# Two-layer hybrid attention block: three engines tied to the planner's order in both attention stages, rotations ahead of the values, a fourth raw weight buffer

## The chip, the core and the metric

The kernel runs on one core of one Trainium2 chip. The metric is device microseconds from the first to the last instruction of one execution. The core's engines are named as in the profile: PE (TensorE: matrix products and transposes), DVE (VectorE), ACT (ScalarE), POOL (GpSimd) and SP (SyncE, which here only issues DMAs). Each engine works through its own list of instructions in the order in which the program gives them; an instruction that waits for another engine holds up everything behind it in its list.

## The reference

512 latent tokens and 256 context tokens, both of width 1024, go through two layers. Each layer modulates its input, runs a token mixer, adds with a gate, normalises, and does the same around a squared-ReLU MLP. Cut to the two mixers:

```python
# layer 0: 16 query heads over 2 key/value heads of 64, a window of 3 blocks of 128 keys plus all 256 context keys
q = apply_rope((hx @ wq)...);  k = apply_rope((hx @ wk)...);  v = (hx @ wv)...
p = softmax_with_sink(concat([s_lat, s_ctx]), sink);  o = p @ [v, vc]

# layer 1: 8 heads of differential attention over 512 + 256 keys; no output for the context tokens
q = apply_rope((hx @ wq).reshape(B, L, H, 2, d)); k = apply_rope(...); v = (hx @ wv).reshape(B, L, H, 2 * d)
p = softmax(s);  a = p[:, :, 0] - lam * p[:, :, 1];  o = a @ v_all
o = o * rsqrt(mean(o * o)) * subln_g * (1 - lam_init)
```

`apply_rope` rotates the two halves of each head of queries and keys by tables of cosines and sines; values are not rotated, and neither is anything of the context tokens.

## The kernel before, in words

Every float32 product is made of three products of rounded numbers: a matrix is split into a high part (ScalarE rounds it) and a low part (VectorE subtracts the high part from the original), and `mm3` (L324) adds high·high, high·low and low·high. So each weight tile is loaded by a DMA into a "raw" buffer, rounded by ScalarE (`w_h`) and subtracted by VectorE (`w_l`, L314): this is `wsplit` (L301). Three raw buffers (`NRAW`, L39) go round; a load waits until the subtraction that last used its buffer is done. The helper `split` (L506) does the same to activations. The helpers `dv`, `ac` and `gp` issue on VectorE, ScalarE and GpSimd, and most of their work stands in the profile under their lines L260, L264 and L268.

**Four stages** follow each other: attention of layer 0, MLP of layer 0, attention of layer 1, MLP of layer 1. The stage of layer 0 starts with the conditioning products (`ada_ps`), key/value projection (`kv_ps`, `kv_job` L1173, `kv_post` L1224), query projection (`q_ps`, `proj` L1284, `q_post` L1255), then 24 groups of 4 heads and one block of 128 tokens (`group`, L1322): scores `s_ps`, VectorE's mask-and-minimum `nm`, ScalarE's exponential, VectorE's reciprocal, GpSimd's scaling, transposes `pT_ps`, product with the values `o_ps`.

The stage of layer 1 goes head by head. `proj1` (L1685) splits the head's four weight tiles and computes, for six blocks of 128 tokens (four latent, two context), `qkv_ps` with queries, keys and values of that head side by side in one PSUM tile. `post1` (L1632) then works on each block: it splits the values into `vt`, rotates queries and keys (`rope`, L488: three VectorE products into `rope` buffers and one GpSimd addition), splits the keys into `sk` and the queries into `sq`, and TensorE transposes them (`kT_ps`, `qT_ps`); ScalarE copies the results to `kS` and `qT`. In the code of before, `post1` issues the split of the values first and the rotation behind it; for a context block there is no rotation, and the split of the values stands ahead of that of the keys. `scores1` (L1746) makes the scores, `nm`, the exponentials `e` and, from the two maps of a head, VectorE's combination `e<-e,nl,e`; `att1` (L1788) transposes it (`pT_ps`), multiplies by the values (`o_ps`), and after each second head scales by the norm (`rms_ps`, `rmsT`, `rmsB`, `rms_bc`; GpSimd's power `rr`). `resid1` (L1716) prepares the residual rows on GpSimd in between.

**What sets the order.** A class `Flow` (L63) is a small planner that runs while the program is built: it keeps a clock of TensorE, a free time per engine and the costs of each operation (`dve`, `act`, `pool2`, and `mm` for a matmul, L221), and picks which job issues its next TensorE work. TensorE's list is exactly what this planner decides (`manual_schedule`, L238). The lists of VectorE, ScalarE and GpSimd are not: the planner simulates them (its rule: of the operations that are ready when the engine comes free, the one issued first), but the framework's own scheduler, with its own costs, decides how they really stand.

PSUM is handed out by two sets of slots (`Slots`, L188): `sS` has 2 slots of two banks, `sm_` has 4 of one bank. A job waits for `ok` (one slot is free) or for `spare` (more than one is). `proj1` asks for `spare` before each block.

Of the kernel before, what the change touches and what calls it, by code (L numbers as in the profile page):

```python
# [19 lines left out]
P = 128  # L20
D = 1024
# [31 lines left out]
class Task:  # L53


    def __init__(self, lat=LAT):
        self.eng, self.us, self.lat = None, 0.0, lat
        self.left, self.at, self.seq = 0, 0.0, 0
        self.kids, self.ring = [], None
        self.done = None  # L60


class Flow:  # L63
# [4 lines left out]
    def __init__(self):  # L68
        self.T = 0.0
        self.jobs = []  # L70
        self.n = 0
        self.free = {"A": 0.0, "D": 0.0, "G": 0.0, "Q": 0.0}
        self.wait = {e: [] for e in self.free}
        self.events = []

# [18 lines left out]
    def op(self, eng, us, deps=(), lat=LAT):  # L94
        t = Task(lat)
        self.n += 1
# [112 lines left out]
def dve(n):  # L209
    return n / 960 + 0.067  # L210
# [10 lines left out]
def mm(n):  # L221
    return max(n / 2400 + 0.003, 0.108)
# [12 lines left out]
def hybrid_block(ctx: ExitStack, tc: tile.TileContext, t: dict, out: bass.AP):  # L235
# [9 lines left out]
    fl = Flow()  # L245
    sS = Slots(fl, 2)
# [12 lines left out]
    def dv(n, deps, fn, lat=LAT, **kw):  # L259
        fn(**kw)  # L260
        return fl.op("D", dve(n), deps, lat)

    def ac(n, deps, fn, lat=LAT, **kw):
        fn(**kw)  # L264
        return fl.op("A", act(n), deps, lat)

    def gp(us, deps, fn, lat=LAT, **kw):
        fn(**kw)  # L268
        return fl.op("G", us, deps, lat)
# [31 lines left out]
    def wsplit(src, n=1024, raw=None, hl=None, pool=False):  # L301
# [7 lines left out]
        a = ac(n, [q, hg], nc.scalar.copy, out=h[:, :n], in_=raw[:, :n])  # L309
        kw = dict(out=l[:, :n], in0=raw[:, :n], in1=f(h)[:, :n], op=ALU.subtract)  # L310
        if pool:
            d = gp(pool2(n), [a], nc.gpsimd.tensor_tensor, **kw)
        else:
            last["split"] = nc.vector.tensor_tensor(**kw)  # L314
            d = fl.op("D", dve(n), [a])
# [217 lines left out]
    def normalise(a, st, dep, lat=LNLAT):  # L533
        mv, rstd, d = moments(st, dep)
        nc.vector.tensor_scalar(out=a, in0=a, scalar1=mv[:, 0:1], scalar2=rstd, op0=ALU.subtract, op1=ALU.mult)
        return fl.op("D", dve(620), [d], lat)
# [44 lines left out]
    def gated_add(pool, give, acc, half, pt, p, gate, last, scale=1.0):  # L581
# [5 lines left out]
        m = fl.op("D", dve(512), [p])  # L587
# [502 lines left out]
    with tc.tile_pool(name="qpool", bufs=6, side="right") as qpool, \  # L1090
# [23 lines left out]
        def start_load(g):  # L1114
# [13 lines left out]
            Wq[0].append(wsplit(t["a_wq"][0, g]))  # L1128
            return Wa, xs


        def start_x(g, xs):
            md = [mod_t[(0, 1, g)], mod_t[(0, 0, g)]]
            for k, xk, q, rr in xs:
# [3 lines left out]
                for s, sl in ((0, slice(0, SEQ)), (1, slice(SEQ, TOK))):  # L1138
                    n = sl.stop - sl.start
                    a = ac(n, [q] + md, nc.scalar.activation, out=hk[:, 0, sl], in_=xk[:, sl], func=AF.Identity,  # L1140
                           scale=sc[:, s:s + 1], bias=sh[:, s:s + 1])
# [3 lines left out]
                    hx_t[k].append(gp(pool2(n), [d], nc.gpsimd.tensor_tensor, **kw) if s else  # L1145
                                   dv(n, [d], nc.vector.tensor_tensor, **kw))
                hx_t[k][1].ring = rr

# [24 lines left out]
        def kv_job():  # L1173
# [15 lines left out]
            setup()  # L1189
            kr4 = qtile(0, "kr4", F32)  # L1190
# [32 lines left out]

        def kv_post(tb, pt, p, kr4):  # L1224
            tok = slice(tb * P, (tb + 1) * P)
            kk_ = pt[:, 0:P].rearrange("p (g d) -> p g d", d=HD)
            vv_ = pt[:, P:2 * P].rearrange("p (g d) -> p g d", d=HD)
# [12 lines left out]
            if tb == NTB - 1:  # L1240
                sm_.give(kvslots[1], r)
# [217 lines left out]

    def need(*lms):  # L1460
        while not all(x in ada_done for x in lms):
            next(filler)
# [148 lines left out]
    with tc.tile_pool(name="attn1", bufs=1, reuse_waits="tile") as pool:  # L1611
        EB1, XB1, SB = 5, 3, 1
        rsk, rsq = Ring(fl, SB), Ring(fl, SB)
# [18 lines left out]
        def post1(hd_, tb, pt, p, give, R):  # L1632
# [6 lines left out]
            _, e = split(P, p, pt[:, 256:384], vt[:, tb, 0], vt[:, tb, 1])  # L1639
            if isx:  # L1640
                qk, e2, r = rope(pool, pt[:, 0:256].rearrange("p (g d) -> p g d", d=HD), tb, 4, p)
                kr = qk[:, 2:4]
                give([e, e2])
            else:
                kr, r = pt[:, P:2 * P].rearrange("p (g d) -> p g d", d=HD), p

# [9 lines left out]
            else:  # L1656
                give([e, d1])
# [26 lines left out]

        def proj1():  # L1685
            for hd_ in range(B_HEADS):
                yield lambda: YES if st["att"] >= hd_ - 2 else NO
                pre = st2["pre"] if hd_ == 0 else {}
                W = st2["W"] if hd_ == 0 else [wsplit(t["b_w"][hd_, u], 768) for u in range(4)]
# [255 lines left out]

    with tc.tile_pool(name="mlp1", bufs=1, reuse_waits="tile") as pool:
# [159 lines left out]
```

## Time and profile before

| what | us |
|---|---|
| median of three runs | 1651.13 (1649.59 to 1657.96) |
| the profiled execution | 1652.57 |
| its span from first to last instruction | 1650.8 |
| PE busy in the span | 1576.2 |
| DVE busy | 1141.4 |
| ACT busy | 794.2 |
| POOL busy | 452.0 |

By tile names the stages of the span lie thus: attention of layer 0 from 0 to about 310 us, its MLP to about 925 us, attention of layer 1 to about 1245 us, and its MLP to the end. The "busy" of a matmul is modelled from its size and matmuls overlap in a pipeline, so a busy PE still has small gaps; an idle PE is idle for certain. In the views of waits, a row names the engine that sat idle, what it then ran, and what released it.

### The profile page before, as it was taken

What the parts mean: (1) busy time and instruction counts of PE and PEld (TensorE: products, weight loads), DVE (VectorE), ACT (ScalarE), POOL (GpSimd) and SP (SyncE); (2) the same over time, 40 slices, a digit from 0 to 9 for tenths busy, and PEclk for the clock granted to TensorE, in tenths of its full rate; (3) what the DMA queues carried; (4) which work ended last, traced back from release to release, by engine and by line L of the source; (5) the groups of instructions that cost most, each with busy time, mean ns of one, the idle gap of its engine ahead of it and who ended that gap; (6) DMA issues with size and microseconds to landing.
All of it is one profiled execution on the core that took longest, in us unless ns stands there. A gap on an engine that the chain in (4) does not pass through costs nothing.

```text
span 1650.8 us, 25195 instructions
## 1 busy us (share of the span) xinstructions
PE 1576.2 (95%) x9465; PEld 1380.7 (84%) x9465; DVE 1141.4 (69%) x2201; ACT 794.2 (48%) x1683; POOL 452.0 (27%) x369
## 2 busy tenths in 40 slices
PE   7899999999999999999997999999989799999998
PEld 5788777789888888889986999899877788888896
DVE  4655676688786768877556777777665886565667
ACT  3465676375343343334416555555552745444550
POOL 1343544106111211221191222220100023233363
PEclk9999999999999999999998999999999999999999
DMA  9110550533344444444423122211122233333321
GB/s 373 43 52 20 192 179 27 187 132 123 101 156 156 146 131 130 163 130 153 153 68 115 49 74 64 75 46 39 49 95 110 93 118 109 103 102 102 99 74 59
DMA packets 66435, 181.18 MB, mean 110 GB/s; under 512 B 7368, under 2 KB 13320, under 8 KB 66312
## 3 DMA queue, kind: packets, MB, share of 16 engines
q1 hardware_dynamic: 66312, 179.56, 32.5%
q8 instruction: 74, 1.21, 0.3%
q14 instruction: 49, 0.40, 0.1%
HBM read 168.49 MB, written 11.04 MB: 109 GB/s over the span
## 4 chain that ended last, share of the span: by engine, by line
PE 69%; DVE 11%; ACT 6%; issue 5%; POOL 5%; DMA 4%; SPq 0%; DVEq 0%; POOLq 0%; ACTq 0%
PE y_ps L325 8%; PE y_ps L326 8%; PE y_ps L327 8%; PE h_ps L325 7%; PE h_ps L326 7%; PE h_ps L327 7%; PE qkv_ps L325 2%; PE qkv_ps L326 2%; PE qkv_ps L327 2%; PE o_ps L1379 2%; PE pT_ps L1397 2%; PE s_ps L1758 2%; POOL acc L268 1%; PE o_ps L1796 1%; DVE w_l L314 1%
## 5 line engine op out<-in xcount | busy, mean ns | idle before, releaser
L325 PE MATMUL y_ps<-w_h,hid 128*128 128x512 f32 (+1 forms) x648 | 255.4, 394 | 1.1 <-DVE fx L260 1.1
L326 PE MATMUL y_ps<-w_l,hid 128*128 128x512 f32 (+1 forms) x648 | 254.6, 393 | 0.9 <-DVE w_l L314 0.9
L327 PE MATMUL y_ps<-w_h,hid 128*128 128x512 f32 (+1 forms) x648 | 254.7, 393 | 0.0
L314 DVE TENSOR_TENSOR w_l<-w_raw,w_h 128x1024 fp32r<-128x1024 f32 (+1 forms) x133 | 160.8, 1219 | 58.9 <-ACT w_h L264 56.8
L264 ACT CAST w_h<-w_raw 128x1024 fp32r<-128x1024 f32 (+1 forms) x133 | 131.7, 1001 | 108.1 <-PE y_ps L327 76.4
L268 POOL TENSOR_TENSOR w_sum<-w_raw 128x512 f32<-128x512 f32 x26 | 59.1, 2274 | 329.0 <-DMA w_raw<-in_w 264.8
L260 DVE TENSOR_TENSOR w_half<-w_raw,w_half 128x512 fp32r<-128x512 f32 x130 | 107.8, 840 | 56.7 <-ACT w_half L264 56.2
L327 PEld LDWEIGHTS y_ps<-w_h,hid 128*128 128x128 f32 x648 | 122.0, 188 | 28.6
L326 PEld LDWEIGHTS y_ps<-w_l,hid 128*128 128x128 f32 x648 | 122.1, 188 | 26.4 <-DVE w_l L314 1.8
L325 PEld LDWEIGHTS y_ps<-w_h,hid 128*128 128x128 f32 x648 | 122.1, 188 | 25.9 <-DVE fx L260 1.5
L264 ACT CAST w_half<-w_raw 128x512 fp32r<-128x512 f32 x130 | 79.1, 621 | 131.8 <-PE h_ps L327 97.1
L325 PE MATMUL qkv_ps<-w_h,hx 128*128 128x384 f32 (+1 forms) x384 | 128.1, 334 | 3.0 <-ACT w_h L264 2.9
L326 PE MATMUL qkv_ps<-w_l,hx 128*128 128x384 f32 (+1 forms) x384 | 123.5, 322 | 1.7 <-DVE w_l L314 1.7
L327 PE MATMUL qkv_ps<-w_h,hx 128*128 128x384 f32 (+1 forms) x384 | 123.2, 321 | 0.0
L268 POOL TENSOR_TENSOR e<-e,sm 128x512 f32<-128x512 f32 (+2 forms) x96 | 92.7, 978 | 109.1 <-DVE sm L260 84.0
L264 ACT ACTIVATE relu<-relu 128x384 f32<-128x384 f32 (+3 forms) x104 | 69.3, 671 | 60.6 <-DVE relu L260 59.4
L260 DVE TENSOR_TENSOR fx<-y_ps,fx 128x512 f32<-128x512 f32 x110 | 75.2, 685 | 33.4 <-PE y_ps L327 33.0
L268 POOL TENSOR_TENSOR rope<-rope,rope 128x256 f32<-128x256 f32 (+1 forms) x40 | 33.9, 847 | 222.7 <-DVE rope L260 175.9
L268 POOL TENSOR_TENSOR w_raw<-w_raw,w_sum 128x512 f32<-128x512 f32 x26 | 39.2, 1508 | 178.3 <-DVE w_half L260 140.7
L673 DVE CUSTOM_DVE_ANT_0 w_raw<-w_raw,cB 128x512 f32<-128x512 f32 x112 | 84.1, 785 | 3.7 <-PE y_ps L327 3.2
L264 ACT ACTIVATE e<-e,nm 128x513 f32<-128x513 f32 (+2 forms) x96 | 65.9, 687 | 32.4 <-DVE nm L260 25.7
L325 PEld LDWEIGHTS qkv_ps<-w_h,hx 128*128 128x128 f32 x384 | 73.0, 190 | 4.8 <-ACT w_h L264 3.3
(268 smaller groups left out, 4323.9 us busy)
## 6 DMA issues: line engine op xcount, KB each, us to landing
w_raw<-in_w SPq DMA_DIRECT2D x128, 512.0 KB, 3.6
w_raw<-in_w_adaT SPq DMA_DIRECT2D x56, 512.0 KB, 3.8
w_raw<-in_w_ada SPq DMA_DIRECT2D x24, 512.0 KB, 3.8
w_raw<-in_b_w SPq DMA_DIRECT2D x32, 384.0 KB, 3.6
raw<-in_w_ada SPq DMA_DIRECT2D x16, 512.0 KB, 9.6
w_raw<-in_a_wq SPq DMA_DIRECT2D x8, 512.0 KB, 7.9
w_raw<-in_a_wo SPq DMA_DIRECT2D x8, 512.0 KB, 4.5
w_raw<-in_b_wo SPq DMA_DIRECT2D x8, 512.0 KB, 4.4
```

Of the source, the lines that this page charges most:

```text
L260: fn(**kw)
L264: fn(**kw)
L268: fn(**kw)
L314: last["split"] = nc.vector.tensor_tensor(**kw)
L325: nc.tensor.matmul(out=o, lhsT=lh, rhs=rh, start=start, stop=False, **kw)
L326: nc.tensor.matmul(out=o, lhsT=lh, rhs=rl, start=False, stop=False, **kw)
L327: last["pe"] = nc.tensor.matmul(out=o, lhsT=ll, rhs=rh, start=False, stop=stop, **kw)
L673: i = fn(**kw)
L1379: nc.tensor.matmul(out=po[odd * HD:odd * HD + HD, 0:256], lhsT=vv[:, kb, kvh], rhs=pt_[:, odd * 256:odd * 256 + 256], start=(i == 0), stop ...
L1397: nc.tensor.transpose(out=pp[:, c * P:(c + 1) * P], in_=es[j][:, i * P:(i + 1) * P], identity=ident)
L1758: nc.tensor.matmul(out=sp[:, c * 512:c * 512 + 384], lhsT=qTt[:, tt, hl, qb * P:(qb + 1) * P], rhs=kS[:, tt, c * 384:c * 384 + 384], start ...
L1796: nc.tensor.matmul(out=po[:, qp * 256:(qp + 1) * 256], lhsT=vt[:, kb, vl], rhs=pt_[:, pl, a * 256:a * 256 + 256], start=(kp == 0 and pl == ...
```

## The change

- **Ties.** `Flow.op` is given the instruction, and while `fl.pin` names an engine, `advance` ties each instruction that had a dependency to the one that the planner ran before it on that engine. The tie is an order alone, not a semaphore. `fl.pin` is "DAG" (VectorE, ScalarE, GpSimd) from the end of the key/value projection to the end of the attention stage of layer 0, and through the attention stage of layer 1. In both MLP stages it is empty. SP's DMAs are not tied.
- **The planner's matmul cost** goes from n/2400 + 0.003 to n/2400 + 0.0135 us.
- **Rotations first.** `post1` issues the rotation (or, of a context block, the split of the keys) ahead of the split of the values, which now depends on the last read of the rotation. `kv_post` of layer 0 copies the values of four blocks by one ScalarE instruction behind the last rotation, and those of the two context blocks by another, where there were six.
- **Fourth raw buffer.** In the stage of layer 1 the fourth weight tile of each head has a raw buffer of its own.
- `proj1` asks for `ok` where it asked for `spare`. At the start, the rounding and subtraction of the last first-half query weight are ordered behind those of the last input block.

```diff
@@ Flow
+            if t.ins is not None and e in self.pin:
+                if e in self.prev:
+                    self.order(t.ins, self.prev[e])
+                self.prev[e] = t.ins
             self.finish(t, s + t.us)
 def mm(n):
-    return max(n / 2400 + 0.003, 0.108)
+    return max(n / 2400 + 0.0135, 0.108)
+    fl.order = lambda i, j: tc.add_manual_dep(i.ins, j.ins.name, ORDER, reason="engine order")
 def dv(n, deps, fn, lat=LAT, **kw):
-        fn(**kw)
-        return fl.op("D", dve(n), deps, lat)
+        return fl.op("D", dve(n), deps, lat, fn(**kw))
@@ start_x
+            if g == 3:
+                for w, x in zip(last["q"], (ia, id_)):
+                    tc.add_manual_dep(w.ins, x.ins.name, ORDER, reason="queue order")
@@ kv_job, behind setup()
+            fl.pin = "DAG"
@@ kv_post
-            e = ac(P, [p], nc.scalar.copy, out=vv[:, tb], in_=vv_)
             if tb < NXB:
                 kr, e, r = rope(pool, kk_, tb, 2, p, [...])
                 if tb == NXB - 1:
-                    sS.give(kvslots[0], e)
+                    sS.give(kvslots[0], v_copy(0, NXB, kvS, e))
@@ post1
-            _, e = split(P, p, pt[:, 256:384], vt[:, tb, 0], vt[:, tb, 1])
             if isx:
                 qk, e2, r = rope(pool, pt[:, 0:256].rearrange("p (g d) -> p g d", d=HD), tb, 4, p)
                 kr = qk[:, 2:4]
-                give([e, e2])
+            def v_split(d):
+                return split(P, d, pt[:, 256:384], vt[:, tb, 0], vt[:, tb, 1])[1]
+            if isx:
+                give(v_split(e2))
...
             else:
-                give([e, d1])
+                give(v_split(d1))
@@ proj1
+        def late_raw():
+            return late.tile([P, 1024], F32, name="w_raw", tag="wh", bufs=1), rlate.get(), rlate
-                W = ... [wsplit(t["b_w"][hd_, u], 768) for u in range(4)]
+                W = ... [wsplit(t["b_w"][hd_, u], 768, late_raw() if u == 3 else None) for u in range(4)]
-                        yield lambda: [sm_.spare, ready2[tb]]
+                        yield lambda: [sm_.ok, ready2[tb]]
```

Three places show what this does to the engines' lists. All counts of instructions stay, but for ScalarE's copies of the values in layer 0 (six before, two now). In both MLP stages the lists are almost those of before.

VectorE, layer 1, before: the norm of the third pair of heads, around which the two context blocks of the next head are worked on (`vt` its values, `sk` its keys) and the weights of the head after it are split (`w_l`); `rr` and `rl` belong to the norm.

```order
L260 SCALAR_TENSOR_TENSOR rr<-rmsT,ep 128x8
L260 TENSOR_TENSOR vt_11435<-qkv_ps,vt_11435 128x128
L260 TENSOR_TENSOR sk<-qkv_ps,sk 128x2x64
L314 TENSOR_TENSOR w_l<-w_raw,w_h 128x768 x3
L260 TENSOR_TENSOR rl<-rmsB,rh 2x512
L260 TENSOR_TENSOR vt_11435<-qkv_ps,vt_11435 128x128
L260 TENSOR_TENSOR sk<-qkv_ps,sk 128x2x64
L314 TENSOR_TENSOR w_l<-w_raw,w_h 128x768
```

The same place of VectorE now.

```order
L267 SCALAR_TENSOR_TENSOR rr<-rmsT,ep 128x8
L267 TENSOR_TENSOR sk<-qkv_ps,sk 128x2x64
L267 TENSOR_TENSOR vt_11431<-qkv_ps,vt_11431 128x128
L267 TENSOR_TENSOR rl<-rmsB,rh 2x512
L319 TENSOR_TENSOR w_l<-w_raw,w_h 128x768 x2
L267 TENSOR_TENSOR sk<-qkv_ps,sk 128x2x64
L319 TENSOR_TENSOR w_l<-w_raw,w_h 128x768
L267 TENSOR_TENSOR vt_11431<-qkv_ps,vt_11431 128x128
L319 TENSOR_TENSOR w_l<-w_raw,w_h 128x768
```

The keys `sk` of each block now stand ahead of its values `vt`; the second block's keys have two weight splits ahead of them instead of three and a `vt`.

ScalarE, start of layer 0, before: `hx` is the modulated input of the last two slices of width 128 (`raw` its source), `w_h` a query weight, `v` the copies of the values, `kstg` the rounding of the rotated keys.

```order
L264 ACTIVATE hx_93<-raw_334,mods_81 128x512
L264 CAST w_h<-w_raw 128x1024
L264 ACTIVATE hx_93<-raw_334,mods_81 128x256
L264 ACTIVATE hx_93<-raw_336,mods_81 128x512
L264 ACTIVATE hx_93<-raw_336,mods_81 128x256
L264 COPY e_799<-nsink 128x1
L264 COPY v_113<-kv_ps 128x128 x2
L264 COPY gate_s<-gate_t 16x128
L264 COPY v_113<-kv_ps 128x128 x2
L264 CAST kstg<-kr_596 128x256
L264 COPY v_113<-kv_ps 128x128
```

The same place of ScalarE now.

```order
L1146 ACTIVATE hx_93<-raw_328,mods_81 128x512
L1146 ACTIVATE hx_93<-raw_328,mods_81 128x256
L1146 ACTIVATE hx_93<-raw_330,mods_81 128x512
L1146 ACTIVATE hx_93<-raw_330,mods_81 128x256
L313 CAST w_h<-w_raw 128x1024
L270 COPY e_792<-nsink 128x1
L270 COPY gate_s<-gate_t 16x128
L270 CAST kstg<-kr_596 128x256 x2
L270 COPY v_113<-kv_ps 128x512
L270 CAST kstg<-kr_596 128x256
```

The weight has moved behind the four inputs, and one copy of the values stands behind the first keys.

VectorE, layer 0, before: the first scores (`ISA e,nm` is the mask-and-minimum of a head's scores) among the query rotations (`rope`, `qstg`).

```order
L260 TENSOR_TENSOR rope_687<-q_ps,c_cosT 128x512
L260 TENSOR_TENSOR qstg<-rope_657,qstg 128x8x64
L260 TENSOR_TENSOR rope_688<-q_ps,c_sinT 128x8x32 x2
L260 TENSOR_TENSOR rope_783<-q_ps,c_cosT 128x512
L260 TENSOR_TENSOR qstg<-rope_687,qstg 128x8x64
L260 TENSOR_TENSOR rope_784<-q_ps,c_sinT 128x8x32 x2
L260 ISA e_799,nm<-s_ps,mask,nsink 128x512
```

The same place of VectorE now.

```order
L267 TENSOR_TENSOR rope_682<-q_ps,c_cosT 128x512
L267 TENSOR_TENSOR qstg<-rope_652,qstg 128x8x64
L267 ISA e_792,nm<-s_ps,mask,nsink 128x512
L267 ISA nm 128x1
L267 TENSOR_TENSOR rope_683<-q_ps,c_sinT 128x8x32 x2
L267 RECIPROCAL sm<-sm 128x1
L267 ISA e_820,nm<-s_ps,mask,nsink 128x512
```

The first mask-and-minimum has moved ahead of the rest of one rotation and of the whole of the next.

More of the change, by code (lines that the diff above doesn't have):

```diff
@@ L74, in __init__ @@
         self.events = []
+        self.prev, self.order, self.pin = {}, None, ""
     def pe(self, us):
@@ L92, in finish, with op @@
             t.ring.back(t.done)
-    def op(self, eng, us, deps=(), lat=LAT):
+    def op(self, eng, us, deps=(), lat=LAT, ins=None):
         t = Task(lat)
+        t.ins = ins if any(d is not None for d in deps) else None
         self.n += 1
@@ L308, in wsplit @@
         q = dma(n, [rg], out=raw[:, :n], in_=src)
-        a = ac(n, [q, hg], nc.scalar.copy, out=h[:, :n], in_=raw[:, :n])
+        last["cast"] = nc.scalar.copy(out=h[:, :n], in_=raw[:, :n])
+        a = fl.op("A", act(n), [q, hg], ins=last["cast"])
         kw = dict(out=l[:, :n], in0=raw[:, :n], in1=f(h)[:, :n], op=ALU.subtract)
@@ L314, in wsplit @@
             last["split"] = nc.vector.tensor_tensor(**kw)
-            d = fl.op("D", dve(n), [a])
+            d = fl.op("D", dve(n), [a], ins=last["split"])
         d.ring = rr
@@ L534, in normalise @@
         mv, rstd, d = moments(st, dep)
-        nc.vector.tensor_scalar(out=a, in0=a, scalar1=mv[:, 0:1], scalar2=rstd, op0=ALU.subtract, op1=ALU.mult)
-        return fl.op("D", dve(620), [d], lat)
+        i = nc.vector.tensor_scalar(out=a, in0=a, scalar1=mv[:, 0:1], scalar2=rstd, op0=ALU.subtract, op1=ALU.mult)
+        return fl.op("D", dve(620), [d], lat, i)
     def ln_job(pool, acc, tb, hx, A, B, ready, st, dep, keep=None, lat=LNLAT):
@@ L1128, in start_load @@
             Wq[0].append(wsplit(t["a_wq"][0, g]))
+            last["q"] = last["cast"], last["split"]
             return Wa, xs
@@ L1139, in start_x @@
                     n = sl.stop - sl.start
-                    a = ac(n, [q] + md, nc.scalar.activation, out=hk[:, 0, sl], in_=xk[:, sl], func=AF.Identity,
-                           scale=sc[:, s:s + 1], bias=sh[:, s:s + 1])
+                    ia = nc.scalar.activation(out=hk[:, 0, sl], in_=xk[:, sl], func=AF.Identity, scale=sc[:, s:s + 1],
+                                              bias=sh[:, s:s + 1])
+                    a = fl.op("A", act(n), [q] + md, ins=ia)
                     d = dv(n // 2, [a], nc.vector.tensor_scalar, out=xk[:, sl], in0=xk[:, sl], scalar1=sc[:, s:s + 1],
@@ L1222, in hybrid_block, with v_copy @@
         xS.free[0:2] = [NO] * 2
+        def v_copy(tb, n, src, p):
+            return ac(n * P, [p], nc.scalar.copy, out=vv[:, tb:tb + n],
+                      in_=src.rearrange("p (b s g d) -> p b s g d", s=2, g=2, d=HD)[:, :, 1])
         def kv_post(tb, pt, p, kr4):
+            kk_ = pt[:, 0:P].rearrange("p (g d) -> p g d", d=HD)
             tok = slice(tb * P, (tb + 1) * P)
-            kk_ = pt[:, 0:P].rearrange("p (g d) -> p g d", d=HD)
-            vv_ = pt[:, P:2 * P].rearrange("p (g d) -> p g d", d=HD)
-            e = ac(P, [p], nc.scalar.copy, out=vv[:, tb], in_=vv_)
             if tb < NXB:
@@ L1240, in kv_post @@
             if tb == NTB - 1:
-                sm_.give(kvslots[1], r)
+                sm_.give(kvslots[1], v_copy(NXB, NTB - NXB, kvm, r))
             yield [r, sm_.ok]
@@ L1458, in hybrid_block @@
         fl.run()
+    fl.pin = ""
     def need(*lms):
@@ L1688, in proj1 @@
                 pre = st2["pre"] if hd_ == 0 else {}
-                W = st2["W"] if hd_ == 0 else [wsplit(t["b_w"][hd_, u], 768) for u in range(4)]
+                W = st2["W"] if hd_ == 0 else [wsplit(t["b_w"][hd_, u], 768, late_raw() if u == 3 else None) for u in range(4)]
                 R = {
```

20 lines of the change are left out of this document (12 added, 8 removed).

## The prediction

> **What bounds the kernel now.** First the page's busy shares and the chain that ended last.
>
> ```profile
> span 1650.8 us, 25195 instructions
> PE 1576.2 (95%) x9465; PEld 1380.7 (84%) x9465; DVE 1141.4 (69%) x2201; ACT 794.2 (48%) x1683; POOL 452.0 (27%) x369
> PE 69%; DVE 11%; ACT 6%; issue 5%; POOL 5%; DMA 4%; SPq 0%; DVEq 0%; POOLq 0%; ACTq 0%
> ```
>
> TensorE is busy for 95% of the span and is 69% of the chain. The change neither adds nor removes a matmul, so all that it can win is TensorE's idle time, and only where it reorders: in the two attention stages. So next a table by stage (columns: length, busy time of PE, its weight loads, DVE, ACT and POOL, then the granted clock).
>
> ```profile
> core 0: us, PE busy (x) PEld busy (x) DVE busy (x) ACT busy (x) POOL busy (x), PEclk, DMA share, GB/s
> 0.00:50.00 50.00, 39.81 (x289) 27.81 (x290) 20.83 (x48) 16.80 (x28) 7.43 (x10) 1.00 0.87 332
> 50.00:310.00 260.00, 251.51 (x1792) 196.86 (x1791) 167.80 (x473) 158.00 (x432) 107.42 (x110) 1.00 0.25 81
> 925.00:1245.00 320.00, 303.75 (x2052) 286.07 (x2052) 227.85 (x471) 175.60 (x406) 58.37 (x70) 0.99 0.19 63
> ```
>
> TensorE idles 320.00 − 303.75 = 16.3 us in the attention of layer 1 and 260.00 − 251.51 = 8.5 us in that of layer 0. No other engine is near full: VectorE is at 71% (227.85 of 320) and 65% (167.80 of 260). What TensorE waits for is the timing of single operations on the others, and this is set by their order. The first 50 us idle for 10.2 us, but there the DMA engines are 87% busy; I grant nothing there. Now who TensorE waits for, in layer 1 (us, times, longest).
>
> ```profile
> PE kT_ps L1662 <- DVE sk L260: 7.1, 5, 2.3
> PE rmsB L1884 <- POOL rr L268: 2.1, 2, 1.0
> PE pT_ps L1824 <- DVE e L260: 1.9, 1, 1.9
> PE s_ps L1758 <- ACT e L264: 1.5, 2, 1.2
> PE pT_ps L1824 <- DVE pT L260: 1.4, 2, 1.0
> PE qkv_ps L326 <- DVE w_l L314: 0.6, 1, 0.6
> PE y_ps L325 <- ACT e L264: 0.5, 1, 0.5
> PE pT_ps L1824 <- ACT kS L264: 0.2, 1, 0.2
> ```
>
> Almost half of these 15.3 us in 15 waits is one kind: the transposes of the keys wait for VectorE's split of the keys. And in layer 0:
>
> ```profile
> PE s_ps L1342 <- DVE nm L260: 2.5, 4, 0.9
> PE q_ps L325 <- DVE rope L260: 1.5, 1, 1.5
> ...
> PE kv_ps L327 <- POOL hx L268: 0.7, 1, 0.7
> ```
>
> The longest of the key waits, instruction by instruction, and the clock behind it:
>
> ```profile
> 1167.26 2.70 DVE L314 TENSOR_TENSOR w_l<-w_raw,w_h 128x768 fp32r<-128x768 f32 x3 [0.47 <-ACT w_h L264]
> 1169.90 0.68 DVE L260 TENSOR_TENSOR rl<-rmsB,rh 2x512 fp32r<-2x512 f32 x1
> 1170.51 0.27 DVE L260 TENSOR_TENSOR vt<-qkv_ps,vt 128x128 fp32r<-128x128 f32 x1
> 1170.87 0.27 ACT L264 CAST sk<-qkv_ps 128x128 fp32r<-128x128 f32 x1 [1.07 <-DVE vt L260]
> 1171.16 0.29 DVE L260 TENSOR_TENSOR sk<-qkv_ps,sk 128x128 fp32r<-128x128 f32 x1 [0.39 <-ACT sk L264]
> 1171.51 0.36 PE L1662 MATMUL kT_ps<-identr,sk 128*128 128x128 f32 x2 [2.32 <-DVE sk L260]
> 1172.60:1179.40 6.80, 6.80 (x20) 5.50 (x19) 4.75 (x7) 2.23 (x4) 0.00 (x0) 0.50 0.34 120
> ```
>
> The keys' rounding on ScalarE is released by VectorE's split of the values, which itself stood behind three weight splits and `rl`. The keys need neither. Right behind the wait the granted clock is 0.50 for 6.80 us, which costs another 3.4 us of TensorE's time.
>
> **Rotations (and keys) first, layer 1.** The ahead-of-the-keys work is seen in two more views: VectorE's and ScalarE's waits in this stage.
>
> ```profile
> DVE vt L260 <- ACT vt L264: 20.7, 14, 4.0
> ...
> ACT sk L264 <- DVE vt L260: 7.1, 12, 1.1
> ...
> ACT w_h L264 <- DMA w_raw<-in_b_w: 2.9, 3, 1.6
> ```
>
> VectorE sits for 20.7 us in front of `vt` and ScalarE for 7.1 us in front of `sk` because of `vt`; both waits lie on the chain from projection to key transposes. The change takes `vt` out of this chain, and the planner's order puts `sk` ahead of `vt` (shown above). Another of the five key waits has a different cause:
>
> ```profile
> 1032.57 1.57 DVE L260 SCALAR_TENSOR_TENSOR e<-e,nl,e 128x768 f32<-128x768 f32 x1
> 1032.60 0.72 POOL L268 TENSOR_TENSOR rs_x<-rs_x,rs_b 128x256 f32<-128x256 f32 x1
> 1034.06 0.28 DVE L260 TENSOR_TENSOR sk<-rope,sk 128x128 fp32r<-128x128 f32 x1
> 1034.48 0.34 PE L1662 MATMUL kT_ps<-identr,sk 128*128 128x128 f32 x2 [1.72 <-DVE sk L260]
> ```
>
> `sk` stood behind a combination of 1.57 us; here only a tie can help. I take 9/10 of the 7.1 us, −6.4, because the first cause is removed outright and the second belongs to the order that TensorE's own list is planned with; what could be late next is the same split behind another long VectorE operation. The throttled stretch goes with its wait, −3.4. The values' PSUM slot is given back later in words, but the same rotation and the same two splits precede the release as before; only their order differs: 0, hidden by the projections of the next block, and if that cover is gone it costs about one `vt` pair, 0.27 + 0.27 = 0.5 us a block.
>
> [...]
>
> **Ties, layer 1.** The other seven rows of waits sum to 8.2 us. The weight wait (0.6) goes with the fourth raw buffer: a fourth load no longer waits for the first subtraction. Of the other 7.6 us I take half, −3.8: each is a wait for an operation that is short and could have stood earlier, but the waits for `e` sit where eight matmuls of scores follow each other faster than ScalarE can serve them, and no order changes that. The stage: −6.4 − 3.4 − 0.6 − 3.8 = −14.2 us. Bounds: 0, and −(16.3 + 3.4) = −19.7.
>
> **Layer 0.** At the start, the weight's rounding and subtraction move behind the last inputs, whose GpSimd part TensorE waited for: −0.7. The six copies of the values leave the front of the key rotations; the row that prices this is VectorE's own wait:
>
> ```profile
> DVE kr L260 <- ACT v L264: 1.7, 2, 1.2
> ```
>
> VectorE begins the rotations 1.7 us sooner, and the 1.5 us that TensorE waits for `rope` behind them shrink by most: −1.2. The scores' waits for `nm` (2.5) lie where a mask-and-minimum stood behind rotations and now stands ahead: −1.5. Together −3.4; bounds 0 and −8.5, all the idle time of the stage.
>
> **What the ties add.** Nothing in the trace shows a tied list, and 0 us is its lower end: no instruction is added. At the upper end the ties make new waits of the kind that stand there now, of which the mean is 15.3/15 = 1.0 us. The planner's costs miss things, as the `e` of 1.57 us beside a GpSimd operation shows; I grant four new waits, +4.0. The planner's new matmul cost shifts only its clock and adds no work of its own: 0, unless jobs now come too early, which is the same +4.0.
>
> **The sum.** −14.2 − 3.4 + 4.0 = −13.6 us on the profiled execution's 1652.57 (span 1650.8 and 1.8 around it), so 1639.0 there; the median of the runs is 1.4 lower, 1651.13, and the forecast is 1651.1 − 13.6 = **1637.5 us**.
>
> **Rival 1: another wait takes the place.** The keys come earlier, but `kS`, the scores and `e` behind them are limited by ScalarE and VectorE, so TensorE waits there. For it: ScalarE waits for `nm` and TensorE for `e` already. Against: both engines are idle for more than a quarter of the stage. Only the throttle and layer 0's waits are won and half of the key waits, less the new ones: −3.4 − 3.4 − 3.5 + 4 = −6.3, about 1645 us.
>
> **Rival 2: the planner's costs are wrong where VectorE and GpSimd meet.** The row that bears on it:
>
> ```profile
> 1021.73 1.00 DVE L260 SCALAR_TENSOR_TENSOR e<-e,nl,e 128x768 f32<-128x768 f32 x1
> L260 DVE SCALAR_TENSOR_TENSOR e<-e,nl,e 128x768 f32<-128x768 f32 x32 | 34.7, 1084 | 0.7
> ```
>
> Alone `e` takes 1.00 us, beside a GpSimd operation 1.57. If the tied order put all 32 beside one, VectorE's 34.7 us would become 32 × 1.57 = 50.2, 15.5 more; were all of it TensorE's, the time would be 1637.5 + 15.5 = 1653.0, no change. Against: VectorE has 92 us free in that stage, and the mean of 1084 ns says that few meet now. [...]
>
> **Rival 3, slower: tied weight casts.** ScalarE's `w_h` casts are tied to the time at which the planner thinks the load has landed. If it lands later, `sk`, `kS` and the exponentials behind the cast stand still, on all 28 loads that seven heads make. ScalarE's three waits for such loads took 2.9 us, 0.97 each; 28 × 0.97 = 27.2 us and one more throttle of 3.4 us, all on TensorE, give 1637.5 + 30.6 = 1668. It decides from (13.6 + 8.3)/28 = 0.8 us a load on. Against: 25 of the 28 casts do not wait now, and the fourth buffer issues a load earlier.
>
> **How the numbers follow.** About 0.5%, 8.3 us, is what a measurement of this kernel can tell from no change. My forecast has 0.65: the causes of the longest waits can be read and the new lists show them gone. Rival 1 has 0.20, rival 2 0.05, rival 3 0.10. The forecast's own low end takes all idle time of both stages and the throttle, 16.3 + 8.5 + 3.4 = 28.2, thus 1623; an estimate of 3 us for gaps that the modelled ends of matmuls hide gives 1620. The high end takes none of the gains and all of the new waits: 1651.1 + 4.0 = 1655. So 1620 to 1655 leaves out rival 3 and a little at the low end. Faster by more than 8.3 us is the forecast, 0.65; within it rivals 1 and 2, 0.25; slower 0.10.
>
> **What would show it.** Right: key-transpose waits for `sk` below 1.5 us in total, no throttled stretch within the attention of layer 1, TensorE idle there below 8 us, and VectorE's wait for `vt` far below 20.7 us. Wrong: TensorE idling as long as before behind other releasers (rival 1), a mean of `e` near 1.5 us (rival 2), ScalarE's waits for `in_b_w` above 20 us (rival 3), or savings in the attention stages that the MLP stages give back.

## The result and the profile after

| | median us | lowest to highest | executions |
|---|---|---|---|
| before | 1653.36 | 1649.59 to 1657.96 | 6 |
| changed | 1643.34 | 1639.20 to 1643.95 | 6 |

The ratio, estimated from all the executions, is 0.9933 (95%: 0.9916 to 0.9951), 11 us less; the two medians lie 10.0 us apart. That is faster by more than the 0.5% that a measurement of this kernel can tell from no change, inside the forecast's range, and about 6 us short of the forecast. Of these 6 us, 2.2 are the starting point: the six executions of before have a median of 1653.36, the three that the forecast started from 1651.13. The profiled execution is the quickest of its six, 1639.2 us; a second profile of the same code (below) took 1644.78 and is nearer to the median. Both are used.

The page of the changed kernel, busy shares and chain:

```profile
span 1637.4 us, 25213 instructions
PE 1571.6 (96%) x9465; PEld 1377.9 (84%) x9465; DVE 1142.4 (70%) x2201; ACT 791.2 (48%) x1679; POOL 433.7 (26%) x369
PE 78%; DVE 9%; ACT 5%; POOL 3%; issue 3%; DMA 2%; SPq 0%; DVEq 0%; ACTq 0%; POOLq 0%
```

TensorE carries 78% of the chain where it carried 69%. Where the time went is read from four places in TensorE's list that every version has: the last `o_ps` of layer 0 (its attention is over), the first `qkv_ps` (layer 1's attention begins), the first `h_ps` of layer 1's MLP, and the last matmul.

| us | before | changed | changed, second profile |
|---|---|---|---|
| start to last `o_ps` of layer 0 | 304.6 | 302.2 | 303.9 |
| from there to the first `qkv_ps` | 587.9 | 590.4 | 595.4 |
| layer 1's attention | 397.4 | 383.6 | 382.9 |
| layer 1's MLP | 352.8 | 353.0 | 352.7 |

The saving is layer 1's attention, 13.8 to 14.5 us. The second row, the stage between the two attention stages, became 2.5 to 7.5 us *longer*. First layer 1, in the window that the prediction used (length, busy time of PE, its weight loads, DVE, ACT, POOL, granted clock):

```profile
925.00:1245.00 320.00, 312.47 (x2129) 294.20 (x2128) 233.80 (x479) 179.49 (x414) 60.34 (x72) 1.00 0.21 70
```

TensorE idles 320.00 − 312.47 = 7.5 us where it idled 16.3, and the mean granted clock is 1.00: no throttled stretch is left there. Its waits in the same window:

```profile
PE s_ps L1785 <- ACT e L270: 2.4, 2, 1.4
PE pT_ps L1851 <- DVE e L267: 1.3, 5, 0.4
PE rmsB L1911 <- POOL rr L273: 1.2, 2, 0.6
PE qT_ps L1699 <- ACT kS L270: 0.7, 1, 0.7
PE qT_ps L1699 <- DVE vt L267: 0.6, 2, 0.3
PE qkv_ps L331 <- DVE w_l L319: 0.5, 1, 0.5
```

The key transposes' row, 7.1 us before, is gone altogether. What is late in its place is small: all rows of the window sum to 7.1 us, against 15.3.

Now the stage that became longer. At its head stands a wait before the transposes of the last token block. TensorE's rows for the last two blocks before, and for the last block changed:

```profile
348.98 1.06 PE L550 MATMUL xn_t<-identr,acc 128*128 128x128 f32 x8 [0.96 <-ACT fx L264]
355.80 1.07 PE L550 MATMUL xn_t<-identr,acc 128*128 128x128 f32 x8 [2.95 <-ACT hx0m L264]
```

```profile
356.46 1.94 PE L555 MATMUL xn_t<-identr,acc 128*128 128x128 f32 x8 [5.17 <-issue]
```

The wait grew from 2.95 to 5.17 us; the block ahead of it, which waited 0.96 us, no longer waits, so 1.3 us are new. The eight transposes behind the wait take 1.94 us instead of 1.07 because they run at half clock (0.50 from 354.3 to 361.1 us). Later in the same stage stands a small transpose of the conditioning gates (`gate_t`). Before, and in the second profile of the changed kernel:

```profile
714.97 0.27 PE L457 MATMUL gate_t<-identr,mods 128*8 128x128 f32 x1
```

```profile
708.44 0.39 PE L332 MATMUL y_ps<-w_h,hid 128*128 128x512 f32 x1
710.88 0.38 PE L462 MATMUL gate_t<-identr,mods 128*8 128x128 f32 x1 [2.04 <-DVE mods L267]
```

It used to start without a wait. Now it stands some forty rows earlier in TensorE's list, ahead of the products on VectorE that make `mods`, and TensorE waits 2.04 us in a stage that neither ties nor rotations touch. What did touch it is the planner's matmul price: in all ten profiled executions that have the new price in this stage (the experiments below included) `gate_t` waits 2.04 to 2.10 us, and in none of the four that have the old one.

### The profile page after: what moved, and what is told of

The parts are those of the page before. It is cut to its first block, busy times and chain, and to the rows that moved or that the text cites. A ratio compares the mean times of both kernels' runs of the same rounds, so it can differ in the third digit from the quotient of the medians.

```text
span 1637.4 us, 25213 instructions
## 1 busy us (share of the span) xinstructions
PE 1571.6 (96%) x9465; PEld 1377.9 (84%) x9465; DVE 1142.4 (70%) x2201; ACT 791.2 (48%) x1679; POOL 433.7 (26%) x369
## 4 chain that ended last, share of the span: by engine, by line
PE 78%; DVE 9%; ACT 5%; POOL 3%; issue 3%; DMA 2%; SPq 0%; DVEq 0%; ACTq 0%; POOLq 0%
PE y_ps L331 9%; PE y_ps L332 9%; PE y_ps L330 9%; PE h_ps L330 7%; PE h_ps L331 7%; PE h_ps L332 7%; PE qkv_ps L330 3%; PE qkv_ps L331 3%; PE qkv_ps L332 3%; PE s_ps L1785 2%; PE o_ps L1395 2%; PE pT_ps L1413 2%; PE o_ps L1823 2%; POOL acc L273 1%; PE q_ps L330 1%
## 5 line engine op out<-in xcount | busy, mean ns | idle before, releaser
L273 POOL TENSOR_TENSOR w_sum<-w_raw 128x512 f32<-128x512 f32 x26 | 42.7, 1643 | 328.0 <-DMA w_raw<-in_w 265.1
```

The source lines that it names most:

```text
L273: return fl.op("G", us, deps, lat, fn(**kw))
```

## Experiments

Each ratio is against the kernel before, run beside it on the same chip. Rows were measured on different chips, on which the median of before lay between 1653.4 and 1656.4 us, so totals are best compared by their ratios. "L1" is the length of layer 1's attention, "between" the stage from layer 0's last `o_ps` to the first `qkv_ps`, both in the one profiled execution of that kernel.

| kernel | median us | ratio (95%) | last `o_ps`, layer 0 | between | L1 |
|---|---|---|---|---|---|
| changed, again | 1643.1 | 0.9934 (0.9909–0.9958) | 303.9 | 595.4 | 382.9 |
| no ties | 1654.2 | 1.0001 (0.9986–1.0015) | 306.4 | 594.6 | 390.2 |
| ties in layer 1 only | 1645.8 | 0.9946 (0.9931–0.9961) | 306.7 | 594.3 | 383.6 |
| VectorE alone tied | 1649.2 | 0.9967 (0.9949–0.9985) | 303.4 | 596.5 | 390.7 |
| ScalarE and GpSimd tied | 1649.1 | 0.9962 (0.9944–0.9980) | 307.0 | 596.1 | 386.1 |
| no ties, values first | 1656.5 | 1.0003 (0.9989–1.0016) | 305.7 | 596.6 | 394.0 |
| three raw buffers | 1647.7 | 0.9951 (0.9933–0.9969) | 303.6 | 592.0 | 389.0 |
| `spare` again | 1648.4 | 0.9955 (0.9939–0.9972) | 302.8 | 593.6 | 387.9 |
| old matmul price | 1636.3 | 0.9891 (0.9875–0.9907) | 297.8 | 588.5 | 387.6 |
| new price in layer 1 only | 1634.7 | 0.9866 (0.9846–0.9886) | 298.9 | 589.7 | 383.4 |
| late scaling | 1640.8 | 0.9915 (0.9898–0.9933) | 304.2 | 594.2 | 383.9 |
| new price in layer 1 only, late scaling | 1631.5 | 0.9863 (0.9837–0.9889) | 298.8 | 586.1 | 383.2 |

### No ties

```diff
-            fl.pin = "DAG"
+            fl.pin = ""
-        fl.prev, fl.pin = {}, "DAG"
+        fl.prev, fl.pin = {}, ""
```

> The changed kernel with no engine tied in either attention stage; the program, rotations first and the fourth raw buffer stay, and so does TensorE's list, row for row. Theory (the saving of some 11 us is layer 1's attention, where the pinned order of VectorE and ScalarE brings the staged keys in time): about half or more of it goes, 1648 to 1654 us, with waits of the key transposes on VectorE's sk of over 3 us back in layer 1 and possibly a stretch at half clock there. Rival A (the order in which the program is written and TensorE's new list give the saving, the ties nothing): 1641 to 1645 us, and key-transpose waits below 1.5 us.

Without ties the change as a whole is worth nothing: 1.0001. TensorE's list is that of the changed kernel row for row, so the ties alone make this difference. Yet my theory is right only in the total. The key-transpose waits do not come back; they are 0.3 us. TensorE waits for other things in layer 1 instead:

```profile
PE s_ps L1785 <- ACT e L270: 5.0, 6, 1.4
PE o_ps L1823 <- DVE pT L267: 3.2, 3, 1.6
PE pT_ps L1851 <- ACT qT L270: 2.3, 2, 1.2
...
PE kT_ps L1684 <- DVE vt L267: 0.3, 1, 0.3
```

So the order of the program (and the list planned with it) cured the keys, and without ties the delay moved on to the exponentials and the transposed probabilities. Layer 1 still gained 397.4 − 390.2 = 7.2 us; the stage between gave back 6.7. No ties with the old matmul price, which (below) is what makes the stage between longer, wasn't tried.

### No ties, values first

Held against the kernel without ties, this undoes the program order in layer 1 alone; the planner's order for TensorE in that stage changes with it.

```diff
+            _, e = split(P, p, pt[:, 256:384], vt[:, tb, 0], vt[:, tb, 1])
             if isx:
                 qk, e2, r = rope(...)
-            def v_split(d):
-                return split(P, d, pt[:, 256:384], vt[:, tb, 0], vt[:, tb, 1])[1]
-                give(v_split(e2))
+                give([e, e2])
...
-                give(v_split(d1))
+                give([e, d1])
```

> The changed kernel without ties and with the values' split ahead of the rotation in layer 1's program again; to be held against the kernel without ties, whose layer-1 attention took 390.2 us against 397.4 before the change. Theory (those 7 us come from the rotations standing first): layer 1's attention 395 to 399 us, 1658 to 1663 us in all, VectorE's vt waiting some 20 us on ScalarE in that stage again. Rival G (they come from the new price and the raw buffer, and the order in the program moves nothing): 389 to 392 us, 1652 to 1656 us.

394.0 lies between the two expectations, so neither is confirmed whole. By the stage's length the order of the program is worth 394.0 − 390.2 = 3.8 us of layer 1 without ties; the totals do not show it (1.0003 against 1.0001). With the values first TensorE idles in the stage as long as before the change, 394.0 − 372.9 = 21.1 us against 397.4 − 375.9 = 21.5. The other 3.4 us of the 7.2 equal what the half-clock stretch behind the key wait cost before (3.4 us), and neither kernel without ties has such a stretch there. The mechanism is seen in TensorE's and VectorE's waits:

```profile
PE kT_ps L1683 <- DVE sk L267: 5.0, 10, 1.4
```

```profile
DVE vt L267 <- ACT vt L270: 23.0, 26, 2.1
```

With the values first, the keys' waits are back, and so is VectorE's wait for `vt`: 20.7 us before the change, 23.0 here, 5.5 in the kernel without ties. Values first *with* ties wasn't tried.

### Which ties

In layer 1 only:

```diff
-            fl.pin = "DAG"
+            fl.pin = ""
```

> The changed kernel with the ties in layer 1's attention alone; TensorE's list is that of the changed kernel. Theory (all of the saving is layer 1's, and the 2 to 4 us that layer 0's attention saves are given back at the head of its MLP): 1641 to 1646 us, within 3 us of the changed kernel, the stage from the first qkv matmul of layer 1 to its MLP's first matmul within 2 us of 384 us. Rival A (ties give nothing in layer 1 and all that they give is in layer 0): 1641 to 1646 us too, but then the kernel without any tie is as fast as this one; the two together decide.

1645.8 lies in the expected band, and layer 1 is at 383.6. The second half of the theory fell: the stage between is as long here (594.3) and without any tie (594.6) as it is with all of them (595.4). So it doesn't "give back" what layer 0 saved; it is longer by itself. Layer 0's ties would be worth 1645.8 − 1643.3 = 2.5 us, but the two intervals overlap, so the total does not show it.

By engine, `fl.pin` set in both stages ("AG" for ScalarE and GpSimd, which were not told apart):

```diff
-            fl.pin = "DAG"
+            fl.pin = "D"
-        fl.prev, fl.pin = {}, "DAG"
+        fl.prev, fl.pin = {}, "D"
```

> The changed kernel with VectorE alone tied in both stages: VectorE's and TensorE's lists are those of the changed kernel row for row, ScalarE's is not. Theory (the waits that ended last in layer 1 name VectorE's results, so its order is the one that counts): 1643 to 1647 us, layer 1's attention 383 to 386 us. Rival H (VectorE itself waits for ScalarE's casts, sk 16 us in that stage, so that ScalarE's order decides): 1649 to 1654 us, layer 1's attention 388 us or more.

> The changed kernel with ScalarE and GpSimd tied and VectorE not: TensorE's and GpSimd's lists are those of the changed kernel and ScalarE's nearly, VectorE's is not. Theory (VectorE's order is the one that counts): 1649 to 1654 us, layer 1's attention 388 us or more, with waits on VectorE's pT or e of over 3 us as in the kernel without ties. Rival H (ScalarE's order decides): 1643 to 1647 us.

The first run's time, 1649.2 us, is what rival H expected, the second's, 1649.1 us, what the theory expected, so neither engine's order decides alone. By the ratios VectorE's ties give about 5.6 of the 11.2 us, those of ScalarE with GpSimd about 6.5, and only both together give all. (Both profiled executions are the slowest of their twelve, and the 390.7 us hold two stretches at half clock, at 1080.7 and 1230.8 us, that cost 3.4 us.) TensorE's waits in layer 1 with VectorE tied and ScalarE free:

```profile
PE pT_ps L1851 <- ACT qT L270: 4.5, 3, 2.0
PE s_ps L1785 <- ACT e L270: 4.1, 5, 1.4
```

and with ScalarE tied and VectorE free:

```profile
PE s_ps L1785 <- ACT e L270: 5.3, 7, 1.4
...
PE o_ps L1823 <- DVE pT L267: 1.0, 2, 0.5
```

In both, one link of the chain scores → `nm` → `e` → transposes is still late. In layer 0 the last `o_ps`, in one profile each, says more for VectorE: 303.4 with its ties, 307.0 with the others, 306.4 without any.

### The fourth raw buffer, and `ok` for `spare`

```diff
-                W = ... [wsplit(t["b_w"][hd_, u], 768, late_raw() if u == 3 else None) for u in range(4)]
+                W = ... [wsplit(t["b_w"][hd_, u], 768) for u in range(4)]
```

> The changed kernel without the fourth raw weight buffer in layer 1's attention (wsplit takes its three raw buffers in turn again). Theory (the buffer is worth the w_l waits that it removes, 0.6 us, and little more): 1643 to 1647 us, layer 1's attention within 2 us of 383.6. Rival E (the buffer matters more, since a cast that waits for a late transfer now holds up everything tied behind it on ScalarE): 1648 to 1656 us, with ScalarE waiting on DMA in layer 1.

```diff
-                        yield lambda: [sm_.ok, ready2[tb]]
+                        yield lambda: [sm_.spare, ready2[tb]]
```

> The changed kernel with layer 1's projection asking for a spare PSUM slot again instead of any free one, as before the change. Theory (that edit is minor): within 3 us of the changed kernel, 1641 to 1647 us. Rival F (it is what lets the projection start early enough for the key transposes): 1648 us or more, with key-transpose waits of over 3 us.

I had both small. Undone, each costs 3 to 5 us: 3.0 and 3.6 by the ratios, 4.4 and 5.1 by the medians, with layer 1 at 389.0 (1.7 of them a half-clock stretch at 1225.1 us) and 387.9. The intervals of the totals overlap that of the changed kernel, so it is layer 1's length and its waits that speak. The planner counts buffers and slots, so TensorE's list in layer 1 changes with each edit, and part of the cost may be that. TensorE's waits over layer 1's attention, with three raw buffers:

```profile
PE qkv_ps L331 <- DVE w_l L319: 4.7, 7, 1.4
```

with `spare` again:

```profile
PE kT_ps L1684 <- DVE sk L267: 3.8, 7, 1.0
PE qkv_ps L331 <- DVE w_l L319: 3.6, 5, 1.4
```

(With the change as it is, `qkv_ps` ← `w_l` is 2.5 us over the same stretch, and key transposes do not appear.) The `spare` rival named the mechanism rightly: a projection that must hold back for a second free slot makes the keys late again, 3.8 us of the 7.1, rotations first and ties notwithstanding. Half of what the buffer's rival named is seen as well, ScalarE waiting on the DMA; that such a cast holds up everything tied behind it isn't shown. ScalarE's waits for weights over layer 1's attention, with three raw buffers and with four:

```profile
ACT w_h L313 <- DMA w_raw<-in_b_w: 3.5, 3, 1.4
```

```profile
ACT w_h L313 <- DMA w_raw<-in_b_w: 0.9, 1, 0.9
```

Its price of 1648 us or more was just not reached; the time lies between the two theories.

### The matmul price

```diff
 def mm(n):
-    return max(n / 2400 + 0.0135, 0.108)
+    return max(n / 2400 + 0.003, 0.108)
```

> The changed kernel with the planner's old price of a matmul (0.003 in place of 0.0135 us beside n/2400), all else as changed, ties too. Theory (ties and rotations first give the saving; the price only shifts where the plan puts vector work between matmuls): 1640 to 1648 us, layer 1's key-transpose waits still below 2 us. Rival B (the plan was late because it thought TensorE faster than it is, and the new price is what mends the waits): 1648 to 1655 us, with waits in layer 1's attention of 12 us or more in place of 7.

Both theories are beaten: 7 us *under* the changed kernel, and the interval ends at 0.9907, where those of the changed kernel start at 0.9916 and 0.9909. The new price helps layer 1 (383 against 387.6 us; 1.7 us of the difference are one half-clock stretch, at 1214.4 us, in the profile with the old price) and costs more elsewhere: the last `o_ps` of layer 0 comes at 297.8 instead of 302.2 to 303.9, and the stage between takes 588.5 instead of 590.4 to 595.4. In that stage `gate_t` is back where it doesn't wait.

So the price was set in layer 1's attention alone (`MM[0]` stands for the constant in `mm`):

```diff
-        fl.prev, fl.pin = {}, "DAG"
+        fl.prev, fl.pin, MM[0] = {}, "DAG", 0.0135
...
-    fl.pin = ""
+    fl.pin, MM[0] = "", 0.003
```

> The changed kernel with the planner's new matmul price (0.0135) in force in layer 1's attention alone and the old one (0.003) everywhere else; ties in both layers. Theory (the new price helps layer 1's attention, 383.6 against 387.6 us from its first qkv matmul to its MLP's first, and hurts layer 0 and the head of its MLP, where the kernel with the old price was 7.6 us ahead by the first y_ps<-hid): the two gains add up, 1631 to 1634 us. Rival D (the old price's gain in layer 0 is paid back in layer 1, so that they cannot be had together): 1636 to 1640 us, with layer 1's attention at 387 us or more.

The stages add up as the theory said, 383.4 us in layer 1 with the rest as under the old price. The median, 1634.7, is just over the expected band, and its interval overlaps that of the old price everywhere (0.9875 to 0.9907), so the total alone would not settle it. Over all profiled executions the stage between took 586.1 to 589.7 us in the four with the old price there (before among them), and 590.4 to 596.6 in the ten with the new one.

### The scaled row at the MLP's head

```diff
             def step(self):
                 tb, self.done = self.done, self.done + 1
+                for b_, i in ((gx, 0), (gc, 1)) if tb == 0 else ():
+                    reload(b_, lnrow[0, i:i + 1])
+                    scale_inplace(b_, ALPHA)
                 d = residual(acc[tb], gx, gc, last["pe"])
...
         def main0():
-            for b_, i in ((gx, 0), (gc, 1)):
-                reload(b_, lnrow[0, i:i + 1])
-                scale_inplace(b_, ALPHA)
```

> The changed kernel with the reload and scaling of layer 0's two residual gains (gx, gc) moved from the end of the output projection to the first residual step of the MLP, so that on VectorE the scaling, which waits 1.06 us for the reloaded row, no longer stands ahead of the last token block's normalisation; TensorE's list is that of the changed kernel. Theory (layer 0's attention saves 2.4 us and the head of the MLP gives it back because of that row): 1.5 to 4 us faster than the changed kernel, 1639 to 1642 us, and the MLP's first y_ps<-hid matmul 1.5 to 4 us sooner than 405.8. Rival C (the gain is given back by something that the MLP waits for anyway, its weights or its normalised rows by another path): within 1 us of the changed kernel, and that matmul still at 405 to 406.

VectorE's list at that place, changed kernel first, then this one:

```profile
351.54 0.68 DVE L267 BATCH_NORM_STATS2 bn<-acc 128x6 f32<-128x512 f32 x1
352.14 0.41 DVE L267 TENSOR_TENSOR hx0m<-fx,hx0m 128x256 fp32r<-128x256 f32 x1
353.61 0.69 DVE L267 TENSOR_SCALAR g<-g 128x1024 f32<-128x1024 f32 x1 [1.06 <-DMA g<-in_lnrow]
354.22 0.20 DVE L267 BATCH_NORM_AGGREGATE mv<-bn 128x2 f32<-128x12 f32 x1
```

```profile
353.95 0.68 DVE L267 BATCH_NORM_STATS2 bn<-acc 128x6 f32<-128x512 f32 x1
354.55 0.41 DVE L267 TENSOR_TENSOR hx0m<-fx,hx0m 128x256 fp32r<-128x256 f32 x1
354.88 0.20 DVE L267 BATCH_NORM_AGGREGATE mv<-bn 128x2 f32<-128x12 f32 x1
```

The statistics are aggregated 354.88 − 353.95 = 0.9 us after they began instead of 354.22 − 351.54 = 2.7, and TensorE's wait for the last block is shorter by as much:

```profile
357.12 1.94 PE L555 MATMUL xn_t<-identr,acc 128*128 128x128 f32 x8 [3.41 <-issue]
```

3.41 us against 5.17 and 5.35 in the two profiles of the changed kernel. That part is shown. The expected milestone was missed (`y_ps<-hid` at 407.5, not before 405.8), and the total, 2.3 us under the changed kernel's median, is inside the overlap of the intervals.

Both together:

> The changed kernel with the new matmul price in layer 1's attention alone and with the scaling of gx and gc moved into the MLP's first residual step. Theory (three savings that do not touch each other: 13.8 us in layer 1's attention, 4 to 7 us in layer 0's, and some 1.8 us in the wait before the last block's transposes at the head of its MLP): 1631 to 1633.5 us, 1 to 3 us under the kernel with the price alone. Rival C (with the old price something else in that head is as late as the scaled row): within 1 us of the kernel with the price alone, 1634 to 1636 us.

This is the fastest version: 1631.5 us, 0.9863 of before (0.9837 to 0.9889), with six executions between 1630.9 and 1632.1. Against the price alone the ratios cannot be told apart; the wait before the last block is 2.82 us where the price alone had 3.94.

### The changed kernel again

> The changed kernel once more, beside these. Theory (its first profiled execution, 1639.2 us, was some 4 us under its other five because the stretch of half clock near 710 us was missing in it): 1642 to 1645 us in the median, and a profiled execution of 1643 us or more shows a half-clock stretch between 640 and 720 us, one of 1639 us or less does not. Rival I (the executions differ in waits and not in the clock): a profiled execution of 1643 us or more without such a stretch.

The median, 1643.1, repeats. The profiled execution, 1644.78 us, has a stretch at half clock at 710.8 us, the one of 1639.2 has none near there, as expected. That is part of the 5.6 us: a stretch of 3.41 us at half clock costs half of that, 1.7, by my estimate. TensorE also idles longer in the stage between, 595.40 − 570.59 = 24.8 us against 590.40 − 568.46 = 21.9, of which 1.2 is one wait for GpSimd's `rstd` near 876 us (2.10 against 0.87). The rest is spread over the first 900 us and wasn't traced further. Why one has it and the other not, at the same wait of 2.04 us, is under the last heading.

## Why the prediction was right or wrong

**Layer 1: right in size, and the parts were not what I took them for.** −14.2 was forecast, −13.8 and −14.5 are measured. The closeness is in part luck: the −14.2 holds none of the new waits, which the forecast counted apart, and the measured figures hold them. The signs that the prediction named are there: key transposes at 0 instead of under 1.5 us, no throttled stretch, 7.5 us of idle time instead of 16.3. VectorE's `vt` row, 20.7 us, fell to 5.5:

```profile
DVE vt L267 <- ACT vt L270: 5.5, 9, 1.2
```

- *Keys, −6.4.* The step named rotations first as the cause, and undoing them brings 5.0 us of the waits back. But undoing the edit that I gave no price at all, `ok` for `spare`, brings 3.8 us back too. The keys need both. The cause for which "only a tie can help" needed no tie: without any the keys' row is 0.3 us.
- *Throttled stretch, −3.4.* Gone with its wait, in both profiles. That is partly chance (last section): the same stage holds a half-clock stretch with the old price (1214.4 us), one with three raw buffers (1225.1 us) and two with VectorE alone tied, where no key wait of 2.3 us is left.
- *Fourth raw buffer, −0.6.* Mis-sized: 3.0 us by the ratios when undone, 5.4 by layer 1's length with a half-clock stretch of 1.7 in it. I priced the one wait that the trace of before showed; with everything else earlier, the weights are what is late next, and I had not asked for that.
- *Ties, −3.8, half of the other waits.* From no ties to all, layer 1 goes from 390.2 to 383.6 or 382.9, so 6.6 to 7.3.

These parts overlap (6.6 for the ties, 5.4 for the buffer and 4.3 for `ok`, each undone alone and read from layer 1's length, already sum to more than the 13.8), because each removes a link of the same chain.

**Layer 0: right direction, partly eaten.** −3.4 was forecast; −2.4 and −0.7 are measured at the last `o_ps`. The three waits that the forecast priced shrank about as it said: those for `hx` (0.7) and for `rope` (1.5) are gone from TensorE's rows, and the scores' waits for `nm` fell from 2.5 to 1.2 us (1.8 in the second profile). Two rows of the transposes of probabilities, 0.6 us before, took back 2.4 us:

```profile
PE pT_ps L1413 <- ACT pT L270: 1.7, 3, 0.7
PE pT_ps L1413 <- POOL e L273: 1.3, 2, 1.2
PE s_ps L1362 <- DVE nm L267: 0.6, 2, 0.3
PE s_ps L1358 <- DVE nm L267: 0.6, 2, 0.4
```

The wait for GpSimd's `e`, 1.3 us, belongs to the new price: it stands in the rows of the kernel without ties too, and not in those of the old price. The added 1.1 us behind ScalarE's `pT` need the tied ScalarE as well: the row is 0.6 us without ties, with VectorE alone tied and with the old price. The waits for `nm` are shortened by the ties (4.2 us without any), and so is the one for `rope`: the forecast put it down to the joined copies of the values, but without ties it is still 1.2 us with the copies joined. What the moved weight gave is open; it was not undone alone.

With the old price the same stage ends 4.4 to 6.1 us sooner, which the prediction did not see.

**The step that failed.** "The planner's new matmul cost shifts only its clock and adds no work of its own: 0, unless jobs now come too early", and before it "only where it reorders: in the two attention stages". The price is used for every matmul, so TensorE's own list changed in layer 0 and in its MLP as well, and jobs did come too early there, the gate's transpose for one. The section on the change calls the lists of the MLP stages almost those of before; with the few rows that differ there, the stage between is 2.5 to 7.5 us longer. I had granted +4.0 for new waits, but inside the attention stages, and there about that much came: in layer 1 `qT_ps` 1.3 us and `s_ps` 0.9 more, in layer 0 `pT_ps` 1.1 and 1.3 more, 4.6 us in all. So the cost in the MLP stood in no term of the sum. The prediction's last sentence on what would show it wrong, savings that the MLP stages give back, happened in part. In the total the misses partly cancel: the two attention stages gained 16.2 and 15.2 us where −13.6 with the new waits was forecast, and the stage between took 2.5 and 7.5 of them.

**The rivals.** Rival 1 did not come: total waits in layer 1 halved. Rival 2: `e` is not 1.57 us long at every meeting with a GpSimd operation. Before, four of the 32 took 1.57 to 1.58 us, each with one beside it for 0.72 to 0.75 us, but two others that met one for 0.43 and 0.85 us took 1.01, and there the GpSimd operations took 1.02 and 1.45 us in place of some 0.73. In the changed kernel eight took 1.42 to 1.59 us, and the mean rose only from 1084 to 1150 ns, 2.1 us on VectorE in all:

```profile
L267 DVE SCALAR_TENSOR_TENSOR e<-e,nl,e 128x768 f32<-128x768 f32 x32 | 36.8, 1150 | 0.8
```

Rival 3 did not come: ScalarE's waits for `in_b_w` in layer 1 are 0.9 us (the row above), not over 20. With three raw buffers they are 3.5, so the fourth buffer is part of why. The range's low end took 3 us for gaps that the modelled ends of matmuls hide; no run shows them, and the lowest time of the changed kernel is 1639.20.

## What to carry to other kernels

When a planner's cost constant changes, compare every engine's list over the whole program, not only in the stage that it was tuned for; here the same constant shortened one stage by some 4 us and made the two ahead of it 6 to 13 us longer (the first `qkv_ps` at 892.6 and 899.3 us instead of 886.3). Setting it per stage kept both gains in the profiles, though the total does not tell it from the old price everywhere. A tied order pays in full only when all engines of the chain are tied: VectorE alone, or ScalarE with GpSimd alone, gave about half and left the delay with the next engine. And price each small edit (a slot rule, one more buffer) for what is late *after* the others have landed; here the two that were priced at 0 and 0.6 us cost 3 to 5 us each when undone.

## What the runs showed of the hardware

Every stretch at half clock (a granted clock of 0.50) that begins and ends between 40 us and the last matmul, in fourteen profiled executions, is 1, 2 or 3 times 3.413 us long (before: 3.413, 6.827 and 10.240), and within one execution all their edges lie on one grid of that period; the phase of the grid differs from execution to execution. I divided each execution into the grid's windows and summed TensorE's idle time in each from the matmul records (at full clock, 40 to 1600 us): all 69 windows with 2.0 us or more of idle time were followed by a window at half clock, none of 6019 with less than 1.0 us, and 22 of 158 between. In the executions of before and of the changed kernel (1639.2 us) alone, it was all 11 windows with 2.02 to 3.01 us, none of 858 with less than 1.0 us and none of 25 between. So in these executions a wait of about 2 us was followed by half clock or not by where it fell on the grid. The `gate_t` wait in the two profiles of the same code, divided at the grid (first the execution of 1639.2, then that of 1644.78):

```profile
702.47:705.88 3.41, 2.28 (x12) 1.66 (x10) 3.07 (x8) 1.52 (x3) 0.00 (x0) 1.00 0.44 131
705.88:709.30 3.42, 2.50 (x12) 2.04 (x13) 1.49 (x5) 0.26 (x1) 0.00 (x0) 1.00 0.59 166
709.30:712.71 3.41, 3.41 (x18) 3.05 (x17) 2.79 (x6) 1.05 (x1) 0.00 (x0) 1.00 0.21 38
```

```profile
707.36:710.77 3.41, 1.48 (x7) 0.85 (x5) 3.15 (x9) 1.52 (x3) 0.00 (x0) 1.00 0.45 154
710.77:714.19 3.42, 3.31 (x9) 2.64 (x10) 0.39 (x2) 0.26 (x1) 0.00 (x0) 0.50 0.44 155
```

In the first, an edge splits the wait into 1.13 and 0.92 us of idle time, and the clock stays at 1.00. In the second nearly all of it, 1.93 us, lies in one window, and the next runs at 0.50.
